# HGRN: logs of the keys added to the running sums of log gates, before the exponentials

## The chip, the cores and the metric

The kernel runs on one core of a Trainium2 chip. The metric is the device time of one execution in microseconds (us). The engines of the core are named as the profile names them: PE (TensorE, matmuls; PEld is its weight load), DVE (VectorE), ACT (ScalarE), POOL (GpSimd) and SP (SyncE, which here only issues DMAs).

## The reference, cut to what matters

The program is one layer of a hybrid encoder: an input projection, three branches (Mamba-2 SSD, RWKV-7, HGRN2), a gated merge, an output projection and a feed-forward net, all in float32 over 1024 positions of width 1024. The change is in the HGRN2 branch, which has 4 heads of 128 channels and two directions.

```
def forget(f):
    ff = lb + (1.0 - lb) * jax.nn.sigmoid(f)
    return heads(jnp.log(ff)), heads(1.0 - ff)          # log gate, key
...
cum = jnp.cumsum(g_c, axis=2)
o_inter = jnp.einsum('bhtk,bhkv->bhtv', q_c * jnp.exp(cum), s)
diff = cum[:, :, :, None, :] - cum[:, :, None, :, :]
decay = jnp.exp(jnp.where(mask, diff, -jnp.inf))
scores = jnp.einsum('bhtsk,bhsk->bhts', q_c[:, :, :, None, :] * decay, k_c)
o_intra = jnp.einsum('bhts,bhsv->bhtv', scores, v_c)
s = (jnp.exp(last[:, :, 0, :])[..., None] * s
     + jnp.einsum('bhsk,bhsv->bhkv', k_c * jnp.exp(last - cum), v_c))
```

So a key k always appears as k times the exponential of a difference of running sums, and since k is positive this can be written as one exponential, with log k inside it.

## The kernel before, in words

Stages follow one another: the RWKV branch, then `hgrn` (about 690 to 1100 us), then `ssd` (1100 to 1462 us), the merges and the feed-forward net. The input projection is cut into jobs of 48 matmuls (`Jobs`, lines L330 to L332, tile `mm`, 128x512), which serve as filling: `J.fill(n)` puts n steps of three matmuls between the pieces of a branch, with fixed numbers in `hgrn` (the table `FILL["hg"]`), and `J.share` deals out what is left over `ssd`. A job also has ACT round its weights (`wh`, L221) and DVE form the remainder (`wl`, L223), and ACT copies the result out (`st`, L272).

The source order is not the order on the engines. A planner in the framework simulates the program when it is built and fixes the order of instructions on each engine by the times that it simulates; only on POOL in a part of `ssd` is it written out by hand. At run time each engine takes its instructions in that fixed order and waits on semaphores.

Per head, `front(hd)` loads the inputs, takes the sigmoids (`gates`), the logs of the gates (`lf`), the keys (`kf`, `kb`: one tile a direction) and the running sums `cf`, `cb` (`cm`, the scans of L1068) and computes level 0. A level halves the blocks (64, 32, ... 1 positions). In `level`, four subtractions of 128x512 fill one tile `lv` of 128x2048 (L1039 on DVE, L1040 to L1042 on POOL), ACT takes one exponential of it (L1043), and DVE multiplies it by q (L1044, 128x1024) and by the two keys (L1045, L1046, 128x512 each). There are three `lv` buffers. `scores` then makes 16 small matmuls (`vps`, shown as 32 in the profile), and DVE merges them into `scd` by a mask (L1162); after the last level POOL copies `scd` to `sc` (L1165), which the output matmuls `ops` (L1179 to L1181) need. The diagonal has its own matmuls `dps` from `ks`, the sum of both keys (L1100), masked into `scd` at L1113. The states at chunk ends use `kd`: a subtraction on POOL (L1123), an exponential (L1124), a product with the key on DVE (L1125), transposes on PE (`tps`, L1085) and copies on ACT (L1086), then `sps` (L1145).

`front(hd + 1)` stands after the last level of head hd, so the planner mixes the next head's scans and levels 0 and 1 or 2 into the last levels of this one. `kf` and `kb` have two buffers each; `cf`, `cb`, `q` and `scd` have one; the tag `t` has six.

Of the kernel before, what the change touches and what calls it, by code (L numbers as in the profile page):

```python
# [9 lines left out]
F32 = mybir.dt.float32  # L10
F32R = mybir.dt.float32r
U8 = mybir.dt.uint8
AF = mybir.ActivationFunctionType
# [16 lines left out]
TB = 6  # L30
# [969 lines left out]
def hgrn(g):  # L1000
    nc, tc, A, J = g.nc, g.tc, g.A, g.J
    V = g.vec
    out = g.dram.tile([4, P, L], F32, tag="out_h", name="out_h")
    with ExitStack() as es:
        hp = es.enter_context(tc.tile_pool(name="h1", bufs=1))
        pp = es.enter_context(tc.tile_pool(name="h1ps", bufs=1, space=PSUM))
        msk = g.msk

        def tl(tag, shape=(P, L), bufs=1, dt=F32):
            return hp.tile(list(shape), dt, tag=tag, name=tag, bufs=bufs)  # L1010

        def gates(hd):

            kf = [tl("kf", bufs=2), tl("kb", bufs=2)]
            gg = tl("gg", bufs=2)
            sg = tl("t", bufs=TB)
            for d in range(2):
                nc.sync.dma_start(kf[d], J.get(g.ph, 4 + 4 * d + hd))
            nc.sync.dma_start(gg, J.get(g.ph, 16 + hd))
            for d in range(2):  # L1020
                nc.scalar.activation(kf[d], kf[d], AF.Sigmoid)
            nc.scalar.activation(sg, gg, AF.Sigmoid)
            nc.gpsimd.tensor_mul(gg, gg, sg)
            explog(g)
            return kf, gg

        def level(i, fr):

            hh = LEV[i]
            G = tl("lv", (P, 2, L), bufs=3)  # L1030

            def v(t):
                return t.rearrange("p (n x h) -> p n x h", x=2, h=hh)
            nb = L // (2 * hh)
            f, b = v(fr.cm[0]), v(fr.cm[1])
            fm = f[:, :, 0, hh - 1:hh].broadcast_to([P, nb, hh])
            bm = b[:, :, 1, 0:1].broadcast_to([P, nb, hh])
            gq, gk = v(G[:, 0]), v(G[:, 1])
            nc.vector.tensor_tensor(gq[:, :, 0], b[:, :, 0], bm, SUB)  # L1039
            nc.gpsimd.tensor_tensor(gq[:, :, 1], f[:, :, 1], fm, SUB)  # L1040
            nc.gpsimd.tensor_tensor(gk[:, :, 0], fm, f[:, :, 0], SUB)
            nc.gpsimd.tensor_tensor(gk[:, :, 1], bm, b[:, :, 1], SUB)  # L1042
            nc.scalar.activation(G, G, AF.Exp)  # L1043
            nc.vector.tensor_mul(G[:, 0], G[:, 0], fr.q)  # L1044
            nc.vector.tensor_mul(gk[:, :, 0], gk[:, :, 0], v(fr.kf[0])[:, :, 0])  # L1045
            nc.vector.tensor_mul(gk[:, :, 1], gk[:, :, 1], v(fr.kf[1])[:, :, 1])  # L1046
            return G

        def front(hd):

            fr = Ctx()
            fr.kf, fr.gg = gates(hd)
            fr.q = tl("q")
            nc.sync.dma_start(fr.q, J.get(g.ph, hd))
            lf = [tl("t", bufs=TB), tl("t", bufs=TB)]
            fr.cm = [tl("cf"), tl("cb")]
            for d in range(2):
                s = fr.kf[d]
                nc.vector.tensor_scalar(s, s, 2.0 ** -63, None, MAX)
                nc.scalar.activation(lf[d], s, AF.Ln, bias=g.lb[:, hd:hd + 1], scale=g.lb1[:, hd:hd + 1])  # L1060

                nc.vector.tensor_scalar(s, s, g.lb1n[:, hd:hd + 1], g.lb1[:, hd:hd + 1], MUL, ADD)
            for d in range(2):

                cs, on, x = fr.cm[d], g.on128[:, d:d + L], lf[d]
                if d == 1:
                    cs, on, x = cs[:, ::-1], on[:, ::-1], x[:, ::-1]
                nc.vector.tensor_tensor_scan(cs, on, x, 0.0, MUL, ADD)  # L1068
            fr.G = level(0, fr)
            return fr  # L1070

        nxt = front(0)
        for hd in range(4):
            fr = nxt
            q, kf, gg, cm = fr.q, fr.kf, fr.gg, fr.cm
            iv = tl("t", bufs=TB)
            nc.sync.dma_start(iv, J.get(g.ph, 12 + hd))
            Vt = tl("Vt", (P, NT, P))
# [14 lines left out]
            for d in range(2):  # L1093
                nc.scalar.activation(E[d], cm[d], AF.Exp)
                J.fill(F[2])

            sc = tl("sc", (P, NT, P))
            scd = tl("scd", (P, NT, 64))
            ks = tl("t", bufs=TB)
            nc.vector.tensor_add(ks, kf[0], kf[1])  # L1100

            def scores(k, q, other, name):

                ps = pp.tile([P, NT, 64], F32, tag="a", name=name, bufs=4)
                for c in range(NT):
                    for b in range(2):
                        s0, t0 = c * P + b * 64, c * P + (b ^ other) * 64
                        nc.tensor.matmul(ps[b * 64:b * 64 + 64, c], k[:, s0:s0 + 64], q[:, t0:t0 + 64],
                                         start=True, stop=True)
                return ps  # L1110

            ps = scores(ks, q, 0, "dps")
            nc.vector.tensor_tensor(scd, ps, g.id64.unsqueeze(1).broadcast_to([P, NT, 64]), MUL)  # L1113
            J.fill(F[4])


            kds, St = [], []
            for d in range(2):
                c3 = cm[d].rearrange("p (c t) -> p c t", t=P)
                last = (P - 1) if d == 0 else 0  # L1120
                kd = tl("t", bufs=TB)
                kd3 = kd.rearrange("p (c t) -> p c t", t=P)
                nc.gpsimd.tensor_tensor(kd3, c3[:, :, last:last + 1].broadcast_to([P, NT, P]), c3, SUB)  # L1123
                nc.scalar.activation(kd, kd, AF.Exp)  # L1124
                nc.vector.tensor_mul(kd, kd, kf[d])  # L1125
                kds.append(kd)
            Gs = [fr.G]
            kts = []
# [5 lines left out]
            for d in range(2):  # L1134
                last = (P - 1) if d == 0 else 0
# [17 lines left out]
            for i in range(7):  # L1153
                G = Gs[0]
                if i < 6:
                    Gs = [level(i + 1, fr)]
                ps = scores(G[:, 1], G[:, 0], i == 0, "vps")
                if i == 0:
                    for b in range(2):
                        nc.scalar.copy(sc[b * 64:b * 64 + 64, :, 64 - b * 64:128 - b * 64], ps[b * 64:b * 64 + 64])  # L1160
                else:
                    nc.vector.copy_predicated(scd, msk[:, i - 1:i, :].broadcast_to([P, NT, 64]), ps)  # L1162
                J.fill(F[7])
# [4 lines left out]
            if hd < 3:  # L1168
                nxt = front(hd + 1)
# [4 lines left out]
            for h in range(2):  # L1174
                ps = pp.tile([P, 4, P], F32, tag="o", name="ops", bufs=1)
                for j in range(4):
                    c = h * 4 + j
# [852 lines left out]
def layer_kernel(ctx, tc, A, out):  # L2030
# [104 lines left out]
```

## Time and profile before

| | us |
|---|---|
| median of 3 runs (lowest, highest) | 2452.01 (2451.94, 2453.88) |
| the profiled execution, its own time | 2453.83 |
| its span, first to last instruction | 2452.1 |
| PE busy / DVE busy / ACT busy / POOL busy | 2288.4 / 1611.1 / 981.5 / 1078.3 |

A busy PE is not a PE at its peak, since the ends of pipelined matmuls are modelled; what counts on PE is where it sits idle and what it then waits for. A timeline row gives the start, the duration, engine, line and operation, and in square brackets the idle time of the engine ahead of it and what ended that. In a row of windows, each engine has its busy time and its number of instructions; PEclk is the TensorE clock granted, 1.00 being full.

### The profile page before, as it was taken

To read this page: it belongs to the slowest core of one execution; us is meant where nothing else is said; L and a number is where in the kernel's file an instruction comes from. 1 tells how busy PE (TensorE), PEld (TensorE's weight loads), DVE (VectorE), ACT (ScalarE), POOL (GpSimd) and SP (SyncE) were. 2 spreads that over 40 slices of the span, in tenths; PEclk is the share of its full clock that TensorE was granted. 3 is DMA by queue.
4 is the path that set the end of the run, shared out by engine and by line. 5 is a ranking of instruction groups with operands and counts; after the bars stand their busy time and mean duration, and the time that the engine had idled before them with its cause. 6 is when DMAs were issued, how large, how long until landed. Compare 5 with 4: busy or idle time off the path is not lost.

```text
span 2452.1 us, 37480 instructions
## 1 busy us (share of the span) xinstructions
PE 2288.4 (93%) x14785; PEld 1847.8 (75%) x14785; DVE 1611.1 (66%) x2069; ACT 981.5 (40%) x1428; POOL 1078.3 (44%) x845
## 2 busy tenths in 40 slices
PE   8998999999988998999899889999899999999895
PEld 6776778788767877878668657788688888877674
DVE  5688763455569578546666776652774454479999
ACT  6554532222454655426224245332433333344333
POOL 4433422443136345310751771421464444447985
PEclk9999999999989999999899989999999999999998
DMA  5455685763442232225645646532232222253311
GB/s 150 122 144 133 165 214 123 223 193 109 148 144 87 87 117 74 80 83 173 148 119 169 146 149 212 191 114 76 61 103 87 78 86 86 79 179 116 100 60 69
DMA packets 381212, 306.23 MB, mean 125 GB/s; under 512 B 111273, under 2 KB 323149, under 8 KB 381037
## 3 DMA queue, kind: packets, MB, share of 16 engines
q1 hardware_dynamic: 260909, 225.71, 31.2%
q10 hardware_dynamic: 119936, 77.61, 10.8%
q8 instruction: 116, 1.90, 0.3%
q0 software_dynamic: 192, 0.52, 0.1%
q14 instruction: 59, 0.48, 0.1%
HBM read 209.68 MB, written 94.11 MB: 124 GB/s over the span
## 4 chain that ended last, share of the span: by engine, by line
PE 61%; DVE 23%; POOL 5%; issue 4%; DMA 3%; ACT 3%; SPq 0%; ACTq 0%; DVEq 0%; POOLq 0%
PE mm L330 7%; PE mm L331 7%; PE mm L332 7%; PE ps L1587 6%; PE ps L1589 6%; PE ps L1588 6%; DVE acc L1926 3%; DVE ab L1804 3%; PE mm L232 2%; PE mm L231 2%; PE mm L233 2%; DVE rb L1804 2%; POOL E L1368 2%; PE Gps L807 1%; DMA E<-cumd 1%
## 5 line engine op out<-in xcount | busy, mean ns | idle before, releaser
L330 PE MATMUL mm<-x,wh 128*128 128x512 f32 (+1 forms) x1232 | 500.1, 406 | 0.6 <-ACT wh L221 0.5
L331 PE MATMUL mm<-x,wh 128*128 128x512 f32 (+1 forms) x1232 | 494.4, 401 | 0.0
L332 PE MATMUL mm<-x,wl 128*128 128x512 f32 (+1 forms) x1232 | 492.3, 400 | 0.0
L330 PEld LDWEIGHTS mm<-x,wh 128*128 128x128 f32 (+1 forms) x1232 | 233.8, 190 | 61.9 <-issue 9.7
L332 PEld LDWEIGHTS mm<-x,wl 128*128 128x128 f32 (+1 forms) x1232 | 233.9, 190 | 55.1 <-issue 4.9
L331 PEld LDWEIGHTS mm<-x,wh 128*128 128x128 f32 (+1 forms) x1232 | 234.1, 190 | 53.7 <-issue 6.2
L1587 PE MATMUL ps<-xb,rb 128*128 128x512 f32 x432 | 168.0, 389 | 0.0
L1588 PE MATMUL ps<-xb,rb 128*128 128x512 f32 x432 | 168.0, 389 | 0.0
L1589 PE MATMUL ps<-xb,rb 128*128 128x512 f32 x432 | 167.9, 389 | 0.0
L1587 PE MATMUL ps<-rb,ab 128*128 128x512 f32 x308 | 125.5, 407 | 20.5 <-DVE acc L1926 19.5
L221 ACT CAST wh<-wr 128x1024 fp32r<-128x1024 f32 (+2 forms) x103 | 100.2, 972 | 101.9 <-PE mm L331 86.2
L223 POOL TENSOR_TENSOR wl<-wr,wh 128x1024 fp32r<-128x1024 f32 x30 | 78.9, 2630 | 133.6 <-ACT wh L221 123.1
L223 DVE TENSOR_TENSOR wl<-wr,wh 128x1024 fp32r<-128x1024 f32 (+2 forms) x73 | 98.5, 1349 | 49.6 <-ACT wh L221 49.4
L1588 PE MATMUL ps<-rb,ab 128*128 128x512 f32 x308 | 122.7, 398 | 2.3 <-POOL rb L1804 2.3
L1589 PE MATMUL ps<-rb,ab 128*128 128x512 f32 x308 | 121.5, 397 | 1.5 <-DVE ab L1804 1.5
L1751 ACT CAST rb<-fs 128x512 fp32r<-128x512 f32 x85 | 52.8, 622 | 166.1 <-PE ps L1589 117.8
L272 ACT COPY st<-mm 128x512 f32<-128x512 f32 x130 | 75.5, 582 | 93.2 <-PE mm L332 81.7
L810 DVE TENSOR_TENSOR Gc<-Gps,mk 128x256 f32<-128x256 f32 x64 | 27.2, 424 | 108.2 <-PE Gps L807 62.1
L231 PE MATMUL mm<-oh,wh 128*128 128x512 f32 x224 | 88.5, 397 | 6.1 <-DVE gt L1491 4.2
L1926 DVE TENSOR_TENSOR acc<-acc,ps 128x512 f32<-128x512 f32 x148 | 94.1, 674 | 0.0
L1588 PEld LDWEIGHTS ps<-xb,rb 128*128 128x128 f32 x432 | 81.1, 188 | 16.9
L1589 PEld LDWEIGHTS ps<-xb,rb 128*128 128x128 f32 x432 | 81.1, 188 | 16.8
(503 smaller groups left out, 5472.0 us busy)
## 6 DMA issues: line engine op xcount, KB each, us to landing
wr<-in_w_in_dram ACTq DMA_DIRECT2D x74, 512.0 KB
fr<-in_ffn_w_in_dram SPq DMA_DIRECT2D x44, 512.0 KB
E<-cumd SPq DMA_DIRECT2D x32, 512.0 KB
pg<-st ACTq DMA_DIRECT2D x48, 256.0 KB
gt<-pg SPq DMA_DIRECT2D x24, 512.0 KB
ad<-a SPq DMA_DIRECT2D x22, 512.0 KB
dr<-in_ffn_w_down_dram SPq DMA_DIRECT2D x22, 512.0 KB
ar<-ad SPq DMA_DIRECT2D x22, 512.0 KB
```

Source lines behind the costliest of these rows:

```text
L221: nc.scalar.copy(hi[:, :kt, :n], raw[:, :kt, :n])
L223: g.lo_eng.tensor_sub(lo[:, :kt, :n], raw[:, :kt, :n], f32(hi[:, :kt, :n]))
L231: nc.tensor.matmul(ps, whi[:, k, :n], xh, start=(k == 0), stop=False)
L272: g.nc.scalar.copy(st[:n], ps)
L330: g.nc.tensor.matmul(ps[:n], w[0][:, k, :n], xh, start=(k == 0), stop=False)
L331: g.nc.tensor.matmul(ps[:n], w[0][:, k, :n], xl, start=False, stop=False)
L332: g.nc.tensor.matmul(ps[:n], w[1][:, k, :n], xh, start=False, stop=(k == KT - 1))
L1587: nc.tensor.matmul(ps, ah, bh, start=(i == 0), stop=False)
L1588: nc.tensor.matmul(ps, ah, bl, start=False, stop=False)
L1589: nc.tensor.matmul(ps, al, bh, start=False, stop=(i == n - 1))
L1804: eng.tensor_sub(blk[:, 1], s, f32(blk[:, 0]))
L1926: nc.vector.tensor_add(m[j], m[j], ps)
```

## The change

For both directions, after `ks` and the diagonal's matmuls, ACT takes the log of the key in place, and DVE subtracts it from the running sum: `ck = cm - log k`, in the key's own tile. A level's two key subtractions use `ck` in place of `cm` on their right side, so the exponential gives the decayed key at once and the products L1045 and L1046 go. The same holds for `kd`: L1125 goes. One of the three subtractions of a level goes from POOL to DVE (L1042). `ks`, `dps` and the masked `scd` move from the head's loop into `front`, since they need the key itself, and the key is capped at 1 - 2^-24 before its log is taken (a second operation in an instruction that was there).

```diff
 (level)
-            f, b = v(fr.cm[0]), v(fr.cm[1])
+            f, b, fk, bk = (v(t) for t in (*fr.cm, *fr.ck))
...
             nc.vector.tensor_tensor(gq[:, :, 0], b[:, :, 0], bm, SUB)
             nc.gpsimd.tensor_tensor(gq[:, :, 1], f[:, :, 1], fm, SUB)
-            nc.gpsimd.tensor_tensor(gk[:, :, 0], fm, f[:, :, 0], SUB)
-            nc.gpsimd.tensor_tensor(gk[:, :, 1], bm, b[:, :, 1], SUB)
+            nc.gpsimd.tensor_tensor(gk[:, :, 0], fm, fk[:, :, 0], SUB)
+            nc.vector.tensor_tensor(gk[:, :, 1], bm, bk[:, :, 1], SUB)
             nc.scalar.activation(G, G, AF.Exp)
             nc.vector.tensor_mul(G[:, 0], G[:, 0], fr.q)
-            nc.vector.tensor_mul(gk[:, :, 0], gk[:, :, 0], v(fr.kf[0])[:, :, 0])
-            nc.vector.tensor_mul(gk[:, :, 1], gk[:, :, 1], v(fr.kf[1])[:, :, 1])
 (front)
-                nc.vector.tensor_scalar(s, s, 2.0 ** -63, None, MAX)
+                nc.vector.tensor_scalar(s, s, 2.0 ** -63, 1 - 2.0 ** -24, MAX, MIN)
...
                 nc.vector.tensor_tensor_scan(cs, on, x, 0.0, MUL, ADD)
+            fr.scd = tl("scd", (P, NT, 64))
+            ks = tl("t", bufs=TB)
+            nc.vector.tensor_add(ks, kf[0], kf[1])
+            ps = scores(ks, fr.q, 0, "dps")
+            nc.vector.tensor_tensor(fr.scd, ps, g.id64..., MUL)
+            for d in range(2):
+                nc.scalar.activation(kf[d], kf[d], AF.Ln)
+                nc.vector.tensor_sub(kf[d], fr.cm[d], kf[d])
+            fr.ck = kf
             fr.G = level(0, fr)
 (the loop over heads)
-            scd = tl("scd", (P, NT, 64))
-            ks = tl("t", bufs=TB)
-            nc.vector.tensor_add(ks, kf[0], kf[1])
-            ps = scores(ks, q, 0, "dps")
-            nc.vector.tensor_tensor(scd, ps, g.id64..., MUL)
...
-                nc.gpsimd.tensor_tensor(kd3, c3[:, :, last:last + 1].broadcast_to([P, NT, P]), c3, SUB)
+                nc.gpsimd.tensor_tensor(kd3, c3[:, :, last:last + 1].broadcast_to([P, NT, P]), ck3, SUB)
                 nc.scalar.activation(kd, kd, AF.Exp)
-                nc.vector.tensor_mul(kd, kd, kf[d])
```

The planner orders the changed program anew, in `hgrn` and `ssd`. Three places matter below. In the changed kernel the lines of these operations are: `dps` L1053, `tps` L1104, the product with q still L1044, the DVE subtractions L1039 and L1042, the subtraction of the log L1086, the masked merge L1163, the scans L1076; in `ssd`, lines are one higher.

First, PE at the first head of `hgrn`, before: the transposes of the values (`tps` x8), the diagonal's matmuls, and the first transposes of `kd` (`tps` x4), with two filling matmuls between each.

```order
L1085 MATMUL tps<-ident,t 128x128 x8
L330 MATMUL mm<-x_208,wh 128x512
L331 MATMUL mm<-x_209,wh 128x512
L1108 MATMUL dps<-q,t 64x64 x16
L332 MATMUL mm<-x_208,wl 128x512
L330 MATMUL mm<-x_217,wh 128x512
L1085 MATMUL tps<-ident,t 128x128 x4
```

The same place in the changed kernel:

```order
L330 MATMUL mm<-x_235,wh 128x512
L1053 MATMUL dps<-q,t 64x64 x16
L1104 MATMUL tps<-ident,t 128x128 x8
L331 MATMUL mm<-x_236,wh 128x512
L332 MATMUL mm<-x_235,wl 128x512
```

The diagonal comes first, ten filling matmuls later than the values' transposes did, and 37 filling matmuls stand between the values' transposes and those of `kd`, where there were four.

Second, DVE in the first head ahead of the product with q of the last level (the last row here), with the next head's scans. Before:

```order
L1162 COPY_PREDICATED scd<-msk,vps 128x512
L1039 TENSOR_TENSOR lv<-cb 128x512
L1162 COPY_PREDICATED scd<-msk,vps 128x512
L1068 SCALAR_TENSOR_TENSOR cf<-on_456,t 128x1024
L1162 COPY_PREDICATED scd<-msk,vps 128x512
L1068 SCALAR_TENSOR_TENSOR cb<-on_456,t 128x1024
L1039 TENSOR_TENSOR lv<-cb 128x8x64
L1162 COPY_PREDICATED scd<-msk,vps 128x512
L1039 TENSOR_TENSOR lv<-cb 128x16x32
L1044 TENSOR_TENSOR lv<-lv,q 128x1024
```

And in the changed kernel:

```order
L1163 COPY_PREDICATED scd<-msk,vps 128x512
L1039 TENSOR_TENSOR lv<-cb 128x512
L1042 TENSOR_TENSOR lv<-cb,kb 128x512
L1163 COPY_PREDICATED scd<-msk,vps 128x512
L1076 SCALAR_TENSOR_TENSOR cb<-on_456,t 128x1024
L1163 COPY_PREDICATED scd<-msk,vps 128x512
L1076 SCALAR_TENSOR_TENSOR cf<-on_456,t 128x1024
L1086 TENSOR_TENSOR kb<-cb,kb 128x1024
L1039 TENSOR_TENSOR lv<-cb 128x8x64
L1039 TENSOR_TENSOR lv<-cb 128x16x32
L1044 TENSOR_TENSOR lv<-lv,q 128x1024
```

The product still stands behind both scans, and now also behind one L1042 and one subtraction of a log. On PE, between this head's level matmuls: before 48 `vps`, 42 filling matmuls, 32 `vps`, 16, 16 `vps`, 37, 16 `vps` and 51 to `ops`; now 48 `vps`, 43, 48 `vps`, 48, 16 `vps`, the next head's `dps`, and 40 to `ops`. The second head has the same; in the third the changed kernel has 32 `vps`, 18, 32 `vps`, 20, 16 `vps`, 26, 32 `vps`.

Third, PE at the end of `ssd`, before:

```order
L1389 MATMUL yo<-S_12085,CT 128x512
L1397 MATMUL st<-xw,Bt 128x512
L1389 MATMUL yo<-S_12086,CT 128x512
L1408 MATMUL yd<-xt,E 128x64 x8
L1397 MATMUL st<-xw,Bt 128x512
L1389 MATMUL yo<-S_12085,CT 128x512
L1397 MATMUL st<-xw,Bt 128x512
L1389 MATMUL yo<-S_12086,CT 128x512
L1408 MATMUL yd<-xt,E 128x64 x8
L1397 MATMUL st<-xw,Bt 128x512
L1389 MATMUL yo<-S_12085,CT 128x512
L1389 MATMUL yo<-S_12086,CT 128x512
```

And in the changed kernel, up to the same last row:

```order
L332 MATMUL mm<-x_427,wl 128x512
L330 MATMUL mm<-x_436,wh 128x512
L331 MATMUL mm<-x_437,wh 128x512
L332 MATMUL mm<-x_436,wl 128x512
L1398 MATMUL st<-xw,Bt 128x512
L1409 MATMUL yd<-xt,E 128x64 x5
L1390 MATMUL yo<-S_12038,CT 128x512
L1409 MATMUL yd<-xt,E 128x64 x3
L1398 MATMUL st<-xw,Bt 128x512
L1390 MATMUL yo<-S_12037,CT 128x512
L1390 MATMUL yo<-S_12038,CT 128x512
```

The filling matmuls had run out before the last chunks, and now reach to the last one. The total of them is 3696 in both. Between the first diagonal and the last normalizing matmul of `hgrn` stand 1085 before and 1005 now (8 of the difference went ahead of it); in `ssd`, 102 stand among the last group's chunks before and 159 now, and 15 more elsewhere.

More of the change, by code (lines that the diff above doesn't have):

```diff
@@ L1040, in level, with scores @@
             nc.gpsimd.tensor_tensor(gq[:, :, 1], f[:, :, 1], fm, SUB)
-            nc.gpsimd.tensor_tensor(gk[:, :, 0], fm, f[:, :, 0], SUB)
-            nc.gpsimd.tensor_tensor(gk[:, :, 1], bm, b[:, :, 1], SUB)
+            nc.gpsimd.tensor_tensor(gk[:, :, 0], fm, fk[:, :, 0], SUB)
+            nc.vector.tensor_tensor(gk[:, :, 1], bm, bk[:, :, 1], SUB)
             nc.scalar.activation(G, G, AF.Exp)
             nc.vector.tensor_mul(G[:, 0], G[:, 0], fr.q)
-            nc.vector.tensor_mul(gk[:, :, 0], gk[:, :, 0], v(fr.kf[0])[:, :, 0])
-            nc.vector.tensor_mul(gk[:, :, 1], gk[:, :, 1], v(fr.kf[1])[:, :, 1])
-            return G
+            return G
+        def scores(k, q, other, name):
+            ps = pp.tile([P, NT, 64], F32, tag="a", name=name, bufs=4)
+            for c in range(NT):
+                for b in range(2):
+                    s0, t0 = c * P + b * 64, c * P + (b ^ other) * 64
+                    nc.tensor.matmul(ps[b * 64:b * 64 + 64, c], k[:, s0:s0 + 64], q[:, t0:t0 + 64],
+                                     start=True, stop=True)
+            return ps
         def front(hd):
             fr = Ctx()
-            fr.kf, fr.gg = gates(hd)
+            kf, fr.gg = gates(hd)
             fr.q = tl("q")
@@ L1057, in front @@
             for d in range(2):
-                s = fr.kf[d]
-                nc.vector.tensor_scalar(s, s, 2.0 ** -63, None, MAX)
+                s = kf[d]
+                nc.vector.tensor_scalar(s, s, 2.0 ** -63, 1 - 2.0 ** -24, MAX, MIN)
                 nc.scalar.activation(lf[d], s, AF.Ln, bias=g.lb[:, hd:hd + 1], scale=g.lb1[:, hd:hd + 1])
@@ L1068, in front @@
                 nc.vector.tensor_tensor_scan(cs, on, x, 0.0, MUL, ADD)
+            fr.scd = tl("scd", (P, NT, 64))
+            ks = tl("t", bufs=TB)
+            nc.vector.tensor_add(ks, kf[0], kf[1])
+            ps = scores(ks, fr.q, 0, "dps")
+            nc.vector.tensor_tensor(fr.scd, ps, g.id64.unsqueeze(1).broadcast_to([P, NT, 64]), MUL)
+            for d in range(2):
+                nc.scalar.activation(kf[d], kf[d], AF.Ln)
+                nc.vector.tensor_sub(kf[d], fr.cm[d], kf[d])
+            fr.ck = kf
             fr.G = level(0, fr)
@@ L1074, in hgrn @@
             fr = nxt
-            q, kf, gg, cm = fr.q, fr.kf, fr.gg, fr.cm
+            q, gg, cm, scd = fr.q, fr.gg, fr.cm, fr.scd
             iv = tl("t", bufs=TB)
@@ L1097, in hgrn @@
             sc = tl("sc", (P, NT, P))
-            scd = tl("scd", (P, NT, 64))
-            ks = tl("t", bufs=TB)
[L1100 to L1110, printed above, removed]
-            ps = scores(ks, q, 0, "dps")
-            nc.vector.tensor_tensor(scd, ps, g.id64.unsqueeze(1).broadcast_to([P, NT, 64]), MUL)
             J.fill(F[4])
@@ L1118, in hgrn @@
             for d in range(2):
-                c3 = cm[d].rearrange("p (c t) -> p c t", t=P)
+                c3, ck3 = (t.rearrange("p (c t) -> p c t", t=P) for t in (cm[d], fr.ck[d]))
                 last = (P - 1) if d == 0 else 0
```

## The prediction

> **What bounds the kernel now.** I read the page first, then the windows of the stage, then what PE waits for there.
>
> ```profile
> span 2452.1 us, 37480 instructions
> PE 2288.4 (93%) x14785; PEld 1847.8 (75%) x14785; DVE 1611.1 (66%) x2069; ACT 981.5 (40%) x1428; POOL 1078.3 (44%) x845
> ...
> 690.00:1100.00 410.00, 372.08 (x2638) 313.09 (x2637) 281.54 (x290) 204.86 (x225) 177.03 (x112) 0.95 0.30 96
> ...
> 750.00:775.00 25.00, 19.94 (x182) 16.38 (x179) 24.96 (x23) 9.80 (x8) 16.84 (x12) 0.93 0.14 43
> 800.00:825.00 25.00, 25.00 (x163) 21.46 (x162) 10.48 (x14) 17.80 (x24) 4.11 (x4) 1.00 0.36 117
> 950.00:975.00 25.00, 18.73 (x153) 14.86 (x151) 24.97 (x20) 8.05 (x7) 16.53 (x11) 0.86 0.21 70
> ```
>
> PE's share over the whole span says only that PE's work is the floor: no matmul is added or taken away, so the change can win only what PE loses. In HGRN that is 410.0 - 372.1 = 37.9 us of idle time, and some half-clock time after it (granted clock 0.95). The loss sits in the levels, where DVE is full (24.96 of 25 us) and PE is not; between heads it is the other way round. The waits of PE in the stage, and its timeline, tell what is late:
>
> ```profile
> PE vps L1108 <- DVE lv L1046: 26.1, 10, 5.2
> PE tps L1085 <- DVE t L1125: 5.6, 1, 5.6
> PE dps L1108 <- DVE t L1100: 4.9, 1, 4.9
> ...
> 717.51 1.98 PE L1108 MATMUL dps<-q,t 128*64 128x64 f32 x32 [4.93 <-DVE t L1100]
> 726.22 1.12 PE L1085 MATMUL tps<-ident,t 128*128 128x128 f32 x4 [5.58 <-DVE t L1125]
> 761.75 0.45 PE L1108 MATMUL vps<-lv 128*64 128x64 f32 x8 [1.34 <-DVE lv L1046]
> 766.62 1.97 PE L1108 MATMUL vps<-lv 128*64 128x64 f32 x32 [3.72 <-DVE lv L1046]
> 784.94 1.15 PE L1108 MATMUL vps<-lv 128*64 128x64 f32 x32 [2.09 <-DVE lv L1046]
> 798.98 0.49 PE L1179 MATMUL ops<-sc,Vt 128*128 128x128 f32 x2 [1.10 <-POOL sc L1165]
> 1049.88 1.97 PE L1108 MATMUL vps<-lv 128*64 128x64 f32 x32 [5.18 <-DVE lv L1046]
> ```
>
> Each of these waits ends on DVE: 10.5 us at the first head's start, 26.1 for level products, 1.1 for the copy before the output. The product that ends the level waits, L1046, is one that the change removes. After 3.7 us of idle time the same 32 matmuls took 1.97 us instead of 1.15: a restart costs that 0.8 and a little more in the matmuls behind it; I take 1.5 us.
>
> **The change, part by part.** What a level's operations cost (shortest, median, longest in ns), and what DVE met at the first head:
>
> ```profile
> L1042 POOL TENSOR_TENSOR lv<-cb x28: 1035/1487/2027, 714.9 to 1049.1; 128x512 f32<-128x512 f32 x28
> L1039 DVE TENSOR_TENSOR lv<-cb x28: 668/1083/1640, 719.7 to 1053.5; 128x512 f32<-128x512 f32 x28
> L1044 DVE TENSOR_TENSOR lv<-lv,q x28: 1208/2056/2136, 728.1 to 1056.8; 128x1024 f32<-128x1024 f32 x28
> L1045 DVE TENSOR_TENSOR lv<-lv,kf x28: 676/686/1572, 730.0 to 1058.0; 128x512 f32<-128x512 f32 x28
> ...
> 711.06 3.87 POOL L1123 TENSOR_TENSOR t<-cf 128x1024 f32<-128x1024 f32 x1
> 713.16 2.31 DVE L1059 TENSOR_SCALAR kf<-kf 128x1024 f32<-128x1024 f32 x1
> 715.40 2.06 DVE L1100 TENSOR_TENSOR t<-kf,kb 128x1024 f32<-128x1024 f32 x1
> 724.05 2.12 DVE L1125 TENSOR_TENSOR t<-t,kf 128x1024 f32<-128x1024 f32 x1
> 731.85 1.21 DVE L1125 TENSOR_TENSOR t<-t,kb 128x1024 f32<-128x1024 f32 x1
> 793.99 0.68 DVE L1059 TENSOR_SCALAR kf<-kf 128x1024 f32<-128x1024 f32 x1
> ```
>
> The same operation takes 1.21 us alone and 2.12 beside POOL; fewer POOL operations therefore also speed up DVE. Per level DVE loses two products (0.69 to 1.57 each) and gains one subtraction (0.67 to 1.64), POOL loses 1.49; over 28 levels that is about 28 x (2 x 1.04 - 1.1) = 27 us less on DVE and 42 us on POOL. The two L1125 a head (1.21) are paid back by the two subtractions of logs, which I price as the same shape, 1.21 to 2.12. ACT gains two logs a head, about 1.1 us each by the exponential below; it has room (204.9 of 410 us busy). The cap on the key joins an instruction that is there and costs nothing.
>
> *First head.* DVE's and ACT's rows:
>
> ```profile
> 710.45 1.28 ACT L1094 ACT_TABLE_LOAD   x1
> 711.75 1.06 ACT L1094 ACTIVATE Ef<-cf 128x1024 f32<-128x1024 f32 x1
> 713.27 1.06 ACT L1094 ACTIVATE Eb<-cb 128x1024 f32<-128x1024 f32 x1
> 721.33 1.91 ACT L1043 ACTIVATE lv<-lv 128x2048 f32<-128x2048 f32 x1 [3.89 <-DVE lv L1039]
> ...
> 743.05 0.39 PE L330 MATMUL mm<-x,wh 128*128 128x512 f32 x1
> 743.28 0.39 PE L331 MATMUL mm<-x,wh 128*128 128x512 f32 x1
> ```
>
> PE came to the values' transposes at about 711.1; ten filling matmuls more (0.23 us from start to start) put the diagonal at 713.4. POOL then has three subtractions only, done by about 712.6, and waits for the logs; so L1059 and the sum of keys run alone (0.68 and 1.21 instead of 2.31 and 2.06) and the sum is there at 714.8: idle 1.4 instead of 4.9. Logs: ACT is free at 714.3, loads a table (1.28), takes both by 717.7; subtractions on DVE to 719.6; POOL's `kd` to about 723, its exponential, behind a second table load and level 0's (1.91), to 725.1. PE wants it after 1.1 + 1.0 of diagonal and transposes and 37 x 0.23, at 725.6: no wait instead of 5.6. The other `kd` and its copies are tight; I add 1.4. Start: 10.5 becomes 2.8, **-7.7**; ends -10.5 (all hidden) and 0 (the two loads and logs come late throughout). The row shows the next ACT instruction 1.30 us after a load began. The Trainium skill ("ScalarE: Activation LUTs", What ACT_TABLE_LOAD costs) adds a drain of about 1.38 us to each switch. With it the two extra loads would cost 2.8 us more and the start would give -4.9; the trace does not agree, since nothing stands between load and exponential.
>
> *Levels.* Count from T, when PE begins the first level.
>
> ```profile
> 771.94 0.72 DVE L1162 COPY_PREDICATED scd<-msk,vps 128x512 f32<-128x512 uint8 x1
> 772.57 2.27 DVE L1068 TENSOR_TENSOR_SCAN cf<-on,t 128x1024 f32<-128x1024 uint8 x1
> ...
> L1165 POOL TENSOR_SCALAR sc<-scd x8: 1488/1654/1959, 795.4 to 1068.5; 64x512 f32<-64x512 f32 x8
> ```
>
> In heads 0 and 1 PE wants the fourth level at T + 3 x 1.15 + 43 x 0.226 = 13.1 (a weight remainder and a product of 128x1024 are priced as L1125, 1.21 or 2.12). DVE does, from about T + 1.4: six half subtractions (6.5), two merges (1.4), two state updates and one product with q outside the levels (2), three level products (1.2 to 2.1 each): the sixth is ready at 16, the fourth at 13.6 to 14.4, so PE waits 1.3. Then PE wants the last level after three levels (3.4) and 48 x 0.23, at 28.7; DVE does a weight remainder (1.2), three merges (2.2), four half subtractions (4.3), two scans (4.5), a log (1.2), and the product beside POOL (2.1): 31.5, a wait of 2.8 (before 2.1). To the output matmuls DVE and POOL need a log, two scalings, two half subtractions, a product, a weight remainder, a merge and two copies, 1.2 + 1.4 + 2.2 + 2.1 + 2.1 + 0.7 + 3.3 = 13.0, PE has 2.2 + 40 x 0.23 = 11.3: 1.8. So 5.9 in each of these heads. The third head's order asks for levels much sooner; the same count gives 3.5 + 0.9 + 4.0 and 1.0 at the output, 9.4. The last has no next head's work in it: 1.3. Together 22.5 against 27.4 (26.1, 1.1 and 0.2 at one state): **-4.9**. Ends: all idle time gone, -27; every DVE operation at its longest, +36 (below). Five restarts instead of seven: **-2** (0 to -8).
>
> *Filling that moves.* 72 filling matmuls, 16.3 us, leave HGRN, since the new order reaches its end with fewer. They are not saved, but 57 go to the end of SSD:
>
> ```profile
> 1428.00:1462.00 34.00, 23.03 (x63) 11.93 (x62) 24.35 (x27) 18.65 (x18) 27.08 (x17) 0.70 0.46 151
> ...
> 1217.55 2.40 DVE L1371 COPY_PREDICATED E<-m,E 128x1024 f32<-128x1024 uint8 x1 [1.19 <-POOL E L1368]
> 1231.64 2.38 DVE L1371 COPY_PREDICATED E<-m,E 128x1024 f32<-128x1024 uint8 x1 [1.19 <-POOL E L1368]
> 1420.12 2.38 DVE L1371 COPY_PREDICATED E<-m,E 128x1024 f32<-128x1024 uint8 x1 [1.19 <-POOL E L1368]
> 1432.87 2.34 DVE L1371 COPY_PREDICATED E<-m,E 128x1024 f32<-128x1024 uint8 x1 [1.19 <-POOL E L1368]
> ```
>
> There PE is idle for 11.0 of 34 us and at clock 0.70, and a chunk takes 12.8 us without filling and 14.1 with it: POOL and DVE set that pace. So 57 x 0.23 = 12.9 us fit in nearly free, say 2 us show; the other 15 cost 3.4. Net -16.3 + 5.4 = **-11**; ends -16 (all hidden) and 0 (all shown). What covers this is POOL's pace in SSD; without that cover the term is 0.
>
> The sum is -7.7 - 4.9 - 2 - 11 = -25.6 us. It is made against the profiled execution (2453.83, span 2452.1); its own time is 1.8 above the median, which I take as the base: 2452.0 - 25.6 = 2426.
>
> **The rivals.** *Only the start is won:* the levels keep their 27 us, since DVE stays the bound and scans and logs still stand ahead of the last product, and the filling shows in SSD: -7.7 and a little, 2442. For it: the full DVE windows. Against it: 27 us less DVE work exactly there. *More:* POOL's relief lets DVE run alone almost always, and all HGRN waits but a few go: -37.9 - 8 - 11, 2395. Against it: the two scans alone are 4.5 us ahead of the last product. *No change:* the time won in HGRN is lost in SSD's new order (its first chunks wait on states, the filling costs 16): 2450. Against it: SSD's pace rows. *Slower:* the two-input operations of DVE all meet POOL, now that a subtraction has moved to DVE. At the longest values of the rows the stretch from T to the last product is 43.5 us, not 31.5: some 11 us more wait in each of three heads and 3 of restarts, +36, so 2462. It decides once that product comes later than T + 40 (25.6 us over three heads). For it: the medians of L1039 and L1044 are nearer the contended end. Against it: POOL has 14 subtractions in that stretch instead of 21. The Trainium skill ("SBUF — State Buffer", Who interferes with whom) says that a two-input DVE instruction and a POOL instruction that reads SBUF exclude each other for a whole instruction. By that rule alone each DVE operation would wait out a POOL one, 0.68 + 1.49 = 2.2 us for the half product; the longest of 28 was 1.57 and the median 0.69, so the trace bears out the conflict, not its full price.
>
> **How the numbers follow.** Chances: forecast 0.65 (its own range 2412 to 2436), only the start 0.17, more 0.08, no change 0.05, slower 0.05. The first two give the range: 2405 to 2445 leaves out 0.18. A measurement here tells 0.2%, 4.9 us, from no change: faster 0.65 + 0.17 + 0.08 = 0.90, same 0.05, slower 0.05.
>
> **What the new profile would show.** PE's wait ahead of the first diagonal about 1 us and none of 5 ahead of the `kd` transposes; level waits of PE ending on L1044, the longest at a head's last level and in the third head; DVE under 260 us and POOL near 135 in HGRN; HGRN over some 30 us sooner; filling (L330) up to the last chunk of SSD, with no idle stretch there. I am wrong if L1044 of the last levels comes as late as T + 40, if ACT's logs hold up the second `kd`, or if SSD grows by the whole 16 us.

## The result, and the profile after

The changed kernel takes 2423.68 us (median of 4 runs, 2419.46 to 2431.26) against 2452.41 us (2451.94 to 2453.88, 4 runs) for the kernel before on the same chip: 0.9885 of it, 95% interval 0.986 to 0.991. The forecast was 2426. The profiled execution took 2423.01 us. Its page begins:

```profile
span 2421.3 us, 37438 instructions
...
PE 2272.7 (94%) x14785; PEld 1838.1 (76%) x14785; DVE 1570.6 (65%) x2041; ACT 988.7 (41%) x1436; POOL 1040.8 (43%) x817
```

The span is 30.8 us shorter with the same 14785 instructions on PE. Where that lies is read from two events per kernel: the last store of HGRN's output, and the first and last state matmul (`st`) of SSD. Rows of one tile's view, first those of before, then those of after (three durations in ns, shortest, median and longest, then the starts of the first and the last one in us):

```profile
L1197 SPq DMA_DIRECT2D out_h<-t x8: 319/320/320, 817.6 to 1098.6; - x8
...
L1397 PE MATMUL st<-xw,Bt x56: 590/592/1222, 1173.3 to 1455.9; 128*128 128x512 f32 x56
```

```profile
L1198 SPq DMA_DIRECT2D out_h<-t x8: 319/320/320, 810.5 to 1061.1; - x8
...
L1398 PE MATMUL st<-xw,Bt x56: 590/593/1168, 1135.2 to 1421.6; 128*128 128x512 f32 x56
```

HGRN ends 37.5 us sooner. Between its first and last `st`, SSD is 286.4 us long instead of 282.6, so 3.8 of the 6.7 us (37.5 - 30.8) that are given back after HGRN are given back there. Between HGRN's end and the first `st` 0.6 us are won. Another 3.5 us are lost behind the last `st`: from there to the end of the span it is 2421.3 - 1421.6 = 999.7 us instead of 2452.1 - 1455.9 = 996.2. The windows of after, the first of them HGRN up to its new end (busy us and instructions of PE, PEld, DVE, ACT, POOL, then the granted clock):

```profile
690.00:1061.00 371.00, 345.87 (x2551) 292.33 (x2550) 242.56 (x259) 212.00 (x229) 140.55 (x84) 0.97 0.31 101
750.00:775.00 25.00, 22.47 (x180) 18.32 (x178) 25.00 (x25) 13.56 (x11) 12.51 (x7) 1.00 0.28 95
1394.00:1428.00 34.00, 26.66 (x108) 17.21 (x106) 24.02 (x25) 15.23 (x17) 23.11 (x16) 1.00 0.49 166
```

PE is idle for 371.0 - 345.9 = 25.1 us in HGRN, where it was idle for 37.9. DVE is still full in the levels (25.00 of 25): the change shortened the stretches in which DVE is the bound, it did not end them. What PE waits for in the stage (total, times, longest):

```profile
PE vps L1053 <- DVE lv L1044: 13.8, 7, 4.9
PE dps L1053 <- DMA q<-ph: 6.9, 3, 2.8
PE dps L1053 <- issue: 2.2, 1, 2.2
PE tps L1104 <- ACT t L1126: 1.4, 2, 0.9
```

The level waits fell from 26.1 us in ten to 13.8 in seven. With two rows of 0.6 and 0.2 that are not shown these make the 25.1. The second row is new: the diagonal's matmuls of heads 1 to 3 now wait for a DMA, the load of `q`. PE's timeline shows how the waits lie:

```profile
713.90 1.15 PE L1053 MATMUL dps<-q,t 128*64 128x64 f32 x32 [2.19 <-issue]
725.38 1.09 PE L1104 MATMUL tps<-ident,t 128*128 128x128 f32 x8 [0.87 <-ACT t L1126]
744.56 2.09 PE L1053 MATMUL vps<-lv 128*64 128x64 f32 x64
758.48 3.33 PE L1053 MATMUL vps<-lv 128*64 128x64 f32 x96 [0.45 <-DVE lv L1044]
775.98 1.15 PE L1053 MATMUL vps<-lv 128*64 128x64 f32 x32 [3.07 <-DVE lv L1044]
779.95 1.98 PE L1053 MATMUL dps<-q,t 128*64 128x64 f32 x32 [2.82 <-DMA q<-ph]
863.99 1.15 PE L1053 MATMUL vps<-lv 128*64 128x64 f32 x32 [3.18 <-DVE lv L1044]
867.86 1.98 PE L1053 MATMUL dps<-q,t 128*64 128x64 f32 x32 [2.72 <-DMA q<-ph]
934.65 1.97 PE L1053 MATMUL vps<-lv 128*64 128x64 f32 x32 [4.89 <-DVE lv L1044]
957.41 1.15 PE L1053 MATMUL dps<-q,t 128*64 128x64 f32 x32 [1.35 <-DMA q<-ph]
1017.16 3.33 PE L1053 MATMUL vps<-lv 128*64 128x64 f32 x96 [0.75 <-DVE lv L1044]
```

Why `q` is late is in the rows of SP and DVE at the first head's end:

```profile
774.72 1.21 DVE L1044 TENSOR_TENSOR lv<-lv,q 128x1024 f32<-128x1024 f32 x1
...
776.00 0.32 SPq L1062 DMA_DIRECT2D q<-ph  x1
```

`q` has one buffer. The product L1044 of the last level is the last reader of the old `q`; it ends at 775.93, SP issues the load at 776.00, and PE goes on at 779.95, some 4 us later. The diagonal used to stand in the loop, long behind this load; it now stands right behind the last level's matmuls, in front of the output's. Last, the operations of a level (shortest, median, longest in ns):

```profile
L1039 DVE TENSOR_TENSOR lv<-cb x28: 670/926/1631, 714.3 to 1021.8; 128x512 f32<-128x512 f32 x28
L1042 DVE TENSOR_TENSOR lv<-cb,kb x28: 677/1545/2032, 719.5 to 1023.1; 128x512 f32<-128x512 f32 x28
L1044 DVE TENSOR_TENSOR lv<-lv,q x28: 1201/1211/1918, 724.4 to 1025.9; 128x1024 f32<-128x1024 f32 x28
```

The subtraction that moved to DVE costs 1.55 us in the median, more than the 1.1 that the prediction took; in return the product with q fell from 2.06 to 1.21.

### The profile page after: what moved, and what is told of

Read it like the earlier page. It is cut to its first block, busy times and chain, and to the rows that moved or that the text cites. A ratio compares the mean times of both kernels' runs of the same rounds, so it can differ in the third digit from the quotient of the medians.

```text
span 2421.3 us, 37438 instructions
## 1 busy us (share of the span) xinstructions
PE 2272.7 (94%) x14785; PEld 1838.1 (76%) x14785; DVE 1570.6 (65%) x2041; ACT 988.7 (41%) x1436; POOL 1040.8 (43%) x817
## 4 chain that ended last, share of the span: by engine, by line
PE 61%; DVE 20%; POOL 5%; DMA 5%; issue 4%; ACT 4%; SPq 1%; ACTq 0%; DVEq 0%; POOLq 0%
PE mm L330 7%; PE mm L331 7%; PE mm L332 7%; PE ps L1588 6%; PE ps L1589 6%; PE ps L1590 6%; DVE ab L1805 3%; DVE acc L1927 2%; PE mm L231 2%; PE mm L232 2%; PE mm L233 2%; DMA E<-cumd 2%; POOL E L1369 2%; DVE rb L1805 1%; PE mm L1588 1%
## 5 line engine op out<-in xcount | busy, mean ns | idle before, releaser
L1588 PE MATMUL ps<-rb,ab 128*128 128x512 f32 x308 | 125.9, 409 | 18.3 <-DVE acc L1927 17.4
L1369 POOL TENSOR_TENSOR E<-E,cums 128x1024 f32<-128x1024 f32 x32 | 69.3, 2178 | 65.5 <-DMA E<-cumd 45.3
L1589 PEld LDWEIGHTS ps<-xb,rb 128*128 128x128 f32 x432 | 81.1, 188 | 16.9
```

The costliest lines, as they stand in the source:

```text
L1369: nc.gpsimd.tensor_tensor(e, e, cs.unsqueeze(2).broadcast_to([P, 8, P]), SUB)
L1588: nc.tensor.matmul(ps, ah, bh, start=(i == 0), stop=False)
L1589: nc.tensor.matmul(ps, ah, bl, start=False, stop=False)
```

## The experiments

Ratios are to the kernel before, run on the same chip (2453.12 us, 2451.88 and 2451.95 in the three groups). Where a kernel keeps the planner's freedom, its order on the engines is a new one each time, so that a difference of two kernels holds the edit and what the planner made of it.

| kernel | us | ratio (95% interval) |
|---|---|---|
| the change | 2423.68 | 0.9885 (0.986, 0.991) |
| before, only L1042 on DVE | 2449.37 | 0.9985 (0.9975, 0.9996) |
| before, only the diagonal early | 2445.68 | 0.9975 (0.9965, 0.9986) |
| before, key products left out, no logs | 2430.95 | 0.9910 (0.9895, 0.9925) |
| before, logs in place of the key products | 2431.79 | 0.9913 (0.9896, 0.9929) |
| the change, L1042 on POOL | 2430.96 | 0.9913 (0.9899, 0.9927) |
| the change, diagonal late | 2421.18 | 0.9874 (0.9858, 0.9891) |
| the change, no logs | 2435.97 | 0.9928 (0.9914, 0.9943) |
| the change, 64 filling matmuls left out | 2421.51 | 0.9872 (0.9857, 0.9887) |
| the change, diagonal late, copies on ACT | 2413.47 | 0.9837 (0.9822, 0.9851) |

**Is the wait for q worth anything?** The changed kernel with the diagonal's matmuls and their mask back in the loop; the sum `ks` stays in `front`.

```diff
 (front)
-            fr.scd = tl("scd", (P, NT, 64))
...
-            ps = scores(ks, fr.q, 0, "dps")
-            nc.vector.tensor_tensor(fr.scd, ps, g.id64..., MUL)
+            fr.ks = ks
 (the loop over heads)
+            scd = tl("scd", (P, NT, 64))
+            ps = scores(fr.ks, q, 0, "dps")
+            nc.vector.tensor_tensor(scd, ps, g.id64..., MUL)
```

> The changed kernel, but the diagonal's matmuls and their mask stand in the loop over heads again, as before the change; the sum of keys and the logs stay in front. Theory (the changed kernel's PE waits 6.9 us, three times, for the load of the next head's q, which has one buffer and is loaded only after the last level's product with q): the three waits and two of its restarts go, 2413 to 2419 us against 2424. Rival (PE then waits for the next late thing, the copy of scores or the next head's transposes): 2421 to 2427.

Measured: 2421.18 us (2417.7 to 2425.01, 5 runs), an interval that overlaps that of the change. PE's waits in this kernel:

```profile
PE vps L1053 <- DVE lv L1044: 15.9, 10, 2.9
PE tps L1102 <- ACT t L1127: 3.3, 1, 3.3
PE ops L1181 <- POOL sc L1167: 3.1, 2, 2.3
PE dps L1053 <- DVE t L1079: 1.7, 1, 1.7
```

The wait for q is gone, and 15.9 + 3.3 + 3.1 + 1.7 = 24.0 us of waits stand in place of 25.1. The rival was right: without the wait for q PE waits for the next late thing. The output's matmuls wait for POOL's copies (3.1), the `kd` transposes at the first head for 3.3, and level waits grow by 2.1.

**Which engine for L1042?** The changed kernel with this subtraction on POOL, and the kernel before with it on DVE.

```diff
-            nc.vector.tensor_tensor(gk[:, :, 1], bm, bk[:, :, 1], SUB)
+            nc.gpsimd.tensor_tensor(gk[:, :, 1], bm, bk[:, :, 1], SUB)
```

> The changed kernel, but the one subtraction of a level that went to DVE (L1042) is on POOL again. Theory (what counts is less DVE and less POOL work that disturbs it; three subtractions in series on POOL hold up each exponential again): slower than the changed kernel, 2428 to 2438 us. Rival (DVE's own list is the bound and each operation taken off it is won): faster, 2410 to 2420 us.

Measured: 2430.96 us (2426.91 to 2432.98, 5 runs), 7.3 more than the change and within the theory's range; the intervals of the two ratios still overlap a little. Its waits, and its product with q:

```profile
PE vps L1053 <- DVE lv L1044: 20.1, 11, 4.1
PE dps L1053 <- DMA q<-ph: 7.2, 3, 3.4
```

```profile
L1044 DVE TENSOR_TENSOR lv<-lv,q x28: 1224/2090/2561, 729.4 to 1037.7; 128x1024 f32<-128x1024 f32 x28
```

Level waits rise from 13.8 to 20.1, and L1044 is at 2.09 us again. The other way round, in the kernel before:

```diff
-            nc.gpsimd.tensor_tensor(gk[:, :, 1], bm, b[:, :, 1], SUB)
+            nc.vector.tensor_tensor(gk[:, :, 1], bm, b[:, :, 1], SUB)
```

> The kernel before with one thing changed: the subtraction L1042 of a level goes from POOL to DVE; no logs, all products with keys stay. Theory (DVE is full in the levels: 28 subtractions of 0.7 to 1.6 us more, but less disturbance by POOL): little, 2446 to 2456 us. Rival (POOL's three subtractions in series were what made levels late): 2432 to 2444 us.

Measured: 2449.37 us (2442.9 to 2454.0, 12 runs), some 3.7 us less than before, as the theory had it.

```profile
L1042 DVE TENSOR_TENSOR lv<-cb x28: 679/1524/1590, 720.9 to 1046.8; 128x512 f32<-128x512 f32 x28
L1044 DVE TENSOR_TENSOR lv<-lv,q x28: 1206/1216/2105, 729.7 to 1051.4; 128x1024 f32<-128x1024 f32 x28
```

Here too L1044 falls to 1.22 us when one subtraction leaves POOL, which pays 0.84 of the 1.52 that DVE takes on; what is left of the gain may lie in POOL's own part, a subtraction of 1.49 us less in each level, or in the planner's new order; no run parts the two. The move is worth a little by itself, and two to three times as much beside the logs (below).

**The diagonal alone.** The kernel before, with `ks`, its matmuls and the mask in `front`.

```diff
 (front, ahead of level 0)
+            fr.scd = tl("scd", (P, NT, 64))
+            ks = tl("t", bufs=TB)
+            nc.vector.tensor_add(ks, fr.kf[0], fr.kf[1])
+            ps = scores(ks, fr.q, 0, "dps")
+            nc.vector.tensor_tensor(fr.scd, ps, g.id64..., MUL)
```

> The kernel before with one thing changed: the sum of keys, the diagonal's matmuls and the mask move into front; no logs, the products with keys stay, L1042 stays on POOL. The planner then gives PE nearly the changed kernel's order at the first head and at the end of SSD (150 filling matmuls among the last group's chunks, 159 in the changed kernel, 102 before). Theory (the start and the filling come from this move, the levels' gain from the logs; the waits for q cost some of it): 2436 to 2446 us. Rival (all comes from fewer products): 2450 to 2460 us.

Measured: 2445.68 us (2442.53 to 2448.75, 10 runs), the upper end of what the theory expected. Its waits:

```profile
PE vps L1055 <- DVE lv L1046: 26.7, 10, 5.7
PE tps L1100 <- DVE t L1124: 5.6, 1, 5.6
PE ops L1178 <- POOL sc L1164: 5.6, 3, 2.2
PE dps L1055 <- issue: 3.3, 1, 3.3
```

The idle time did not fall (41.2 us here, 37.9 before); the wait ahead of the `kd` transposes is 5.6 us as it was. The 6 to 7 us came from elsewhere: this kernel has 1027 filling matmuls in HGRN where before has 1085, and HGRN ends at 1088.1 instead of 1098.6. So the order that the planner makes of the moved diagonal takes filling out of HGRN, which SSD then hides. The change's gain at the start hardly comes from the earlier diagonal: of the 10.5 us of waits there, 8.9 (5.6 and 3.3) are still paid here.

**The products, and the price of the logs.** The kernel before, with the key products taken out and nothing in their place:

```diff
-            nc.vector.tensor_mul(gk[:, :, 0], gk[:, :, 0], v(fr.kf[0])[:, :, 0])
-            nc.vector.tensor_mul(gk[:, :, 1], gk[:, :, 1], v(fr.kf[1])[:, :, 1])
...
-                nc.vector.tensor_mul(kd, kd, kf[d])
```

> The kernel before with only the products with the keys left out (two per level and two per head; the key's factor is left out of levels and chunk ends), no logs, nothing moved: what the removal alone is worth. Theory (DVE's list in the levels is the bound, 27 us of waits there): 2432 to 2440 us against 2452. Rival (POOL's three subtractions in series stay and the levels stay late): 2444 to 2452.

Measured: 2430.95 us (2424.01 to 2433.74, 5 runs), a little under the theory's range, far from the rival's. So 21 of the 29 us come when only the products go. Not all of it need be theirs: this kernel too has a new order, and HGRN, which ends 26.4 us sooner (1072.2), holds 48 filling matmuls fewer, 10.9 us; its level waits fell by 8.3 us (26.1 to 17.8). What a new order gives with all products in place is known for one order only, that of the kernel with the early diagonal: 6 to 7 us. Then the same with the logs and their subtractions in (the changed kernel with both moves undone, that is the edits of the first and the second experiment together):

> The logs and the key's products alone: the kernel before, with the key products replaced by the logs and their subtractions as in the changed kernel, but the diagonal's matmuls in the loop and L1042 on POOL, as before. Set beside the run with the products left out and no logs (0.991), it gives the price of the logs: 8 logs on ACT, 8 subtractions of 128x1024 on DVE, 2 table loads more. Theory (the logs' work lies in the levels' windows, where DVE is full, so it is paid at 8 x 1.21 to 2.12 us less what the transposes' products L1125 gave back in both): slower than that run by 3 to 10 us, 2434 to 2441 against 2452 for the kernel before, level waits about 20 us. Rival (the logs fall into the time between levels and are free): within 3 us of it, 2428 to 2434. Second rival (the planner's order decides): outside of both ranges.

Measured: 2431.79 us (2425.8 to 2434.34, 6 runs); its ratio 0.9913 beside 0.9910, so in the whole time the logs cost nothing that can be told, and the first rival was right. The window 690 to 1060 us and the level waits, first without logs, then with them:

```profile
690.00:1060.00 370.00, 342.18 (x2536) 288.78 (x2535) 210.25 (x220) 192.27 (x210) 172.05 (x112) 0.98 0.30 99
...
PE vps L1106 <- DVE lv L1044: 17.8, 11, 2.2
```

```profile
690.00:1060.00 370.00, 342.94 (x2486) 287.11 (x2485) 227.66 (x226) 205.48 (x221) 189.39 (x112) 0.96 0.30 99
...
PE vps L1053 <- DVE lv L1044: 17.8, 10, 3.3
```

In this window DVE is busy for 17.4 us more, ACT for 13.2, and POOL for 17.3 with the same 112 instructions, and PE's level waits stay at 17.8 us. But HGRN is not equally long in the two: its last store is issued at 1072.2 without the logs and at 1083.5 with them. Filling makes up about half of that, 23 matmuls or 5.2 us; for the rest there is only the granted clock, 0.96 in the window instead of 0.98. Behind HGRN the difference shrinks, to 7.5 us at the last `st` (1430.4 and 1437.9) and 3.4 at the end of the spans. So it is shown that the whole time does not tell the logs, and not shown that they are free inside HGRN.

With this kernel the two moves can be read apart, each with and without the other, as far as the new orders let one: L1042 on DVE is worth 0.9913 to 0.9874 with the diagonal late, and 0.9913 to 0.9885 with it early, 7 to 10 us; only with the diagonal late are the two intervals apart. The early diagonal is worth nothing with L1042 on POOL (0.9913 both), and 0.9874 to 0.9885 with it on DVE, 2.5 us the wrong way with overlapping intervals.

**The logs, taken out of the change.** The changed kernel without logs and their subtractions.

```diff
-                nc.scalar.activation(kf[d], kf[d], AF.Ln)
-                nc.vector.tensor_sub(kf[d], fr.cm[d], kf[d])
-            fr.ck = kf
+            fr.ck = fr.cm
```

> The changed kernel without the two logs and the two subtractions of logs per head: the running sums themselves go into the levels and the chunk ends, so the key's factor is left out of the computation. It prices the logs alone. Theory (each log's subtraction stands on DVE ahead of a last level's product, and the first head waits for a table load and the logs): 2414 to 2420 us against 2424. Rival (the logs lie beside other work and cost nothing): 2421 to 2427.

Measured: 2435.97 us (2427.62 to 2437.99, 6 runs). Both theories missed it: with less work the kernel is 12 us slower than the change. PE's waits, the first diagonal's matmuls (ns per matmul: shortest, median, longest; then the starts of the first and the last), and what DVE and POOL do just before them:

```profile
PE vps L1053 <- DVE lv L1044: 10.9, 3, 4.4
PE dps L1053 <- DMA q<-ph: 7.8, 3, 3.5
PE dps L1053 <- issue: 5.1, 1, 5.1
...
L1053 PE MATMUL dps<-q,t x32: 314/314/369, 716.6 to 718.3; 128*64 128x64 f32 x32
...
713.60 2.91 DVE L1080 TENSOR_TENSOR t<-kf,kb 128x1024 f32<-128x1024 f32 x1
713.10 2.34 POOL L1124 TENSOR_TENSOR t<-cb 128x1024 f32<-128x1024 f32 x1
```

The same two engines at the same place in the change:

```profile
712.59 1.21 DVE L1080 TENSOR_TENSOR t<-kf,kb 128x1024 f32<-128x1024 f32 x1
717.42 4.92 POOL L1041 TENSOR_TENSOR lv<-cf,kf 128x512 f32<-128x512 f32 x1 [5.31 <-DVE kf L1086]
```

The waits come to 32.2 us (with 4.0, 3.5 and 0.9 in rows not shown) instead of 25.1, in fewer and longer pieces, and after the long ones matmuls take 314 ns instead of the 222 of the change's first diagonal. The cause of the 5.1 us is in the rows. PE comes to the first diagonal at 711.5 (716.6 - 5.1), and at 711.7 in the change (713.9 - 2.2). But the sum of keys that the diagonal needs takes 2.91 us here, beside POOL's subtractions, and ends at 716.51. In the change POOL stands idle for 5.3 us until a log's subtraction is done, the sum runs alone in 1.21 us and ends at 713.80. So at the first head the logs help, by holding POOL back. The pair above agrees: there the sum takes 2.06 us without the logs and 1.21 with them, and the wait ahead of the first diagonal is 4.5 us and 0.3. In this kernel the longer wait is 2.9 of the 12 us, and the slower matmuls behind it come on top. What made the other waits longer is not shown. The planner put filling and transposes elsewhere, and no run holds its order.

**The filling at SSD's end.** The changed kernel, with 64 filling matmuls of the last two jobs left out, which stood among SSD's last chunks (64 x 0.226 = 14.5 us of PE).

```diff
 (Jobs.steps)
+                cut = i >= len(self.jobs) - 2
...
+                if not cut:                   (matmuls 2 and 3 of a step)
...
```

> The changed kernel with 64 filling matmuls left out: the last two jobs keep one of their three products, which leaves a part of two gate columns' projection out. The order up to the end of SSD stays. 64 x 0.226 = 14.5 us of PE work. Theory (the filling that the change moved to the end of SSD is hidden behind the pace of POOL and DVE there): 2419 to 2424 us. Rival (it lies on the path): 2408 to 2411.

Measured: 2421.51 us (2418.77 to 2422.26, 4 runs), 2 to 3 us less than the change, with overlapping intervals. The row of `st`:

```profile
L1400 PE MATMUL st<-xw,Bt x56: 590/592/1221, 1136.7 to 1423.9; 128*128 128x512 f32 x56
```

Without this filling SSD is 287.2 us long, and 286.4 with it. It is hidden, as the prediction had it; that the pace is that of POOL and DVE agrees with this.

**What is left at a head's end.** The first experiment's kernel, with POOL's copies of the scores on ACT.

```diff
-                nc.gpsimd.tensor_scalar(sc[...], scd[...], 1.0, None, MUL)
+                nc.scalar.copy(sc[...], scd[...])
```

> The kernel with the diagonal back in the loop (2421 us), and the two copies of the scores ahead of a head's output go from POOL to ACT. Theory (the 3.1 us of waits ahead of the output matmuls go, and POOL's 3.3 us a head disturb DVE no more): 2413 to 2418 us. Rival (the last level's product stays the late thing): 2419 to 2423.

Measured: 2413.47 us (2407.7 to 2414.96, 4 runs). It is the fastest of all, and its interval lies below that of the change.

```profile
PE vps L1053 <- DVE lv L1044: 13.2, 11, 2.8
PE ops L1180 <- ACT sc L1167: 6.9, 3, 4.6
PE tps L1102 <- ACT t L1127: 3.1, 1, 3.1
...
690.00:1060.00 370.00, 346.46 (x2560) 291.98 (x2559) 235.91 (x262) 216.81 (x240) 133.04 (x82) 0.99 0.31 103
```

The time came out as the theory had it, but not by its wait: the waits ahead of the output grew from 3.1 us to 6.9, now behind ACT's copies, and all waits together are hardly fewer (23.2 us, against 24.0 in the first experiment's kernel). HGRN ends at 1052.2 instead of 1065.5. From 690 us on it holds 37 filling matmuls fewer (1086 instead of 1123), 8.4 of those 13.3 us, and its granted clock is 0.99 instead of 0.97. Whether the faster clock comes from the copies or from the new order is not shown.

## Why the prediction was right, point by point

The forecast of 2426 with 2412 to 2436 held, and so did the mechanism in the main: fewer two-input operations on DVE (242.6 us busy in HGRN, under 260 as said), fewer on POOL (140.6, near 135), less idle time on PE. By its terms:

- *First head: idle 10.5 to 2.8, -7.7.* Measured 10.5 to 4.2 (2.19 and 0.87 in the timeline above, 0.58 ahead of a second `tps`, 0.57 ahead of `sps`), -6.3. The second `kd` was the uncertain part, as said. None of 5 us is left ahead of the `kd` transposes, as forecast. The first diagonal waited 2.2 us, not 1.4, for the sum of keys (712.59 + 1.21 = 713.80 in the rows of the experiment without logs). That this sum would run alone, with POOL waiting for the logs, was worked out rightly: without the logs it took 2.91.
- *Levels: 27.4 to 22.5.* Measured 20.9 us, but the parts are others. The level waits were to be 17.9 (4.1 in each of heads 0 and 1, 8.4, and 1.3) and are 13.8: 3.07 and 3.18 at the last levels, where 2.8 was worked out (the last product ends 31.4 us after T, from 744.56 to 775.93, and 31.5 was the sum of its rows), 4.89 and 0.72 in the third head instead of 8.4. The waits at the outputs were to be 4.6 and are none. The 6.9 us for q were not foreseen. The step that failed is "To the output matmuls ... PE has 2.2 + 40 x 0.23 = 11.3": the 2.2 took the next head's diagonal for work that PE can do at once. The text on the kernel says that `q` has one buffer, and the prediction put the diagonal behind the last level's L1044 without asking when its own `q` could be loaded. That the total came out nevertheless is partly luck, since 8.7 us too much in two parts met 6.9 too little in a third. It agrees with the first experiment, where another wait is paid in place of that for q. One reading of the rows was wrong as well: the prediction says that each of PE's waits ends on DVE, but the 1.1 us ahead of the output ended on POOL's copy (`POOL sc L1165`).
- *L1042 at 1.1 us.* It was mis-sized: 1.55 in the median. L1044 at 2.1 was mis-sized the other way: 1.21. The row of before (1208/2056/2136) showed both values, and the relief of POOL should have been put on this operation above all.
- *Five restarts for seven, -2.* Three are left, at 779.95, 867.86 and 934.65. Of the 37.5 us in HGRN, 12.8 are idle time and 16.3 the 72 filling matmuls; the other 8.4 are a remainder. Some 1.6 of it lie ahead of the stage, since at 690 us the changed kernel has done 7 filling matmuls more (1697 instead of 1690). The rest goes with the granted clock of the stage, 0.97 instead of 0.95, that is with matmuls that ran slower before. The term was mis-sized by some 5 us: four restarts went and not two, which at its own price of 1.5 us each would already be 6.
- *Filling that moves, -16.3 + 5.4.* Measured -16.3 and 6.7 given back. Only 3.8 of these are in SSD, so the cover that was named (POOL's and DVE's pace there) hid a little more than was said, which the kernel with 64 filling matmuls fewer bears out. The 3.5 behind the last `st` have no cause that a run shows: that stretch takes 994.1 to 1001.4 us in the kernels here, and none of the edits lies in it. But "no idle stretch there" was wrong: PE is idle for 7.3 of the last 34 us, at clock 1.00 now, where before it was idle for 11.0 at 0.70.

In sum -6.3, -6.5, -8.4, -16.3 and +6.7 give -30.8 of the span, against -25.6; the medians differ by 28.7.

The rivals: *only the start* fails, since leaving out the products gave 21 us, and the levels' idle time fell. *Slower by contention* fails, since the last product comes at T + 31.4, not T + 40. *No change* fails, since 6.7 of the 37.5 us were given back, and not all. *More* (2395) was bounded as said: DVE is still full in the levels.

## What to carry to other kernels

Where a full engine sets the waits, taking elementwise products off it by folding the factor into an exponent can pay (here 21 of 29 us came with the products, the new order included), and no price of the logs showed in the whole time. When work is moved ahead in a program, ask of each operand with one buffer when its last reader lets go. And where a planner orders the program, compare variants by waits and granted clock as well as by time: taking the logs out cost 12 us here, in part because an engine that they had held back then ran beside DVE.

## What the runs showed of the hardware that was not expected

The product with q of 128x1024 took about 2.06 us (median) whenever POOL had three subtractions of a level (2056 in the kernel before, 2057 without key products, 2090 in the change with L1042 on POOL), with the one exception of 1677 in the kernel with logs and late diagonal; it took 1211 to 1219 with two on POOL, in six kernels. So the median went with one POOL operation more or less in a level. The Trainium skill ("SBUF — State Buffer", Who interferes with whom) says that a DVE instruction with two SBUF inputs contends with a POOL instruction that reads SBUF. These medians agree with that.

How long a wait may be before matmuls run slower behind it was not one number. In the change 32 matmuls took 1.15 us after 3.07 and 3.18 us of idle time, but 1.98 after a second wait of 2.82 and 2.72 that followed 1.15 us of work later. In the change with L1042 on POOL a single wait of 2.82, after filling without a gap, was enough:

```profile
715.81 1.97 PE L1053 MATMUL dps<-q,t 128*64 128x64 f32 x32 [2.82 <-issue]
```

The Trainium skill ("TensorE: Matmul & The Clock Gate", What's actually happening) tells of a window of about 3.4 us that runs freely, and of half the clock after one that was idle. A window that runs freely agrees with unlike outcomes of like waits, and the 1.97 us after 4.89 in the third head agrees too. But a wait of 2.82 us after gapless work is shorter than such a window and was followed by the slow matmuls all the same; there the measurement decides, and how the window's phase lay no run here shows.
